# A mixture-of-experts layer whose experts' tokens are gathered two experts at a time

## The chip, the cores and the metric

The kernel runs on one core of a Trainium2 chip. The metric is device time in microseconds (us) of one execution. The core has five engines that run their own instruction queues: TensorE (PE in the profile; its weight loads are listed as PEld), VectorE (DVE), ScalarE (ACT), GpSimd (POOL) and SyncE (SP, which here only issues DMAs). TensorE's clock has two levels, 1.2 and 2.4 GHz; the profile gives the granted share of the higher one.

## The reference

Two transformer blocks of two layers each, on 256 tokens of 1024 channels, in float32. The change is in the second layer of the first block, whose feed-forward is a mixture of eight experts, two for each token:

```
def moe_swiglu(h, router_w, w1, w3, w2):
    logits = h @ router_w
    top_v, top_i = lax.top_k(logits, 2)
    probs = softmax(top_v)
    gates = sum(one_hot(top_i, 8) * probs[..., None], axis=-2)
    y = zeros_like(h)
    for e in range(8):
        y = y + gates[..., e:e + 1] * ((silu(h @ w1[e]) * (h @ w3[e])) @ w2[e])
    return y
```

w1 and w3 are 1024 x 2816 for each expert, w2 is 2816 x 1024.

## The kernel before

**Weights.** Every product is made of three: a float32 operand is held as a high and a low part of type fp32r, and `mm3` (lines 212 to 216) adds high x high, high x low and low x high. The weights arrive as float32 and are split on the core. `wload` (192 to 201) takes a staging slot, issues a 512 KB DMA on SyncE (line 198), casts the piece to its high part on ScalarE (199) and subtracts on VectorE to get the low part (200). There are six slots of split weights (`wh`, `wl`), and staging slots of two kinds: five (`ws`) for the whole kernel, and eleven more (`wx`) while the mixture layer runs. `stage` (181 to 187) hands them out in turn, by a counter `turn` that is set to 13 before the layer (line 1476). A staging slot is free again once the subtraction of line 200 has read it.

**Experts.** The one-hot matrix of an expert, tokens by slots, picks at most 128 tokens for the main pass. `collect(e)` makes these one-hot columns on VectorE (`select`, line 799, tile `pmr`), and `gather` (818 to 828) multiplies the tokens, held by rows as a high part (`hTh`) and a low part (`hTl`), with them: 8 channel blocks x 2 blocks of tokens x 2 parts are 32 matmuls with 128 moving columns, in two PSUM banks. The two banks go to `sink` (854 to 859): ScalarE applies the norm's scale and shift, one instruction for each channel block (858), and `split` makes the high and low part (lines 238 and 239). The result is held in a pair of four `y4` buffers, so that two experts' tokens are held at a time. `place` and `dispatch` (803 to 816) transpose the one-hot columns for the way back and make the gates.

**Order.** The loop of lines 915 to 933 goes over the experts and, in each, over six groups of hidden units (five of 512, one of 256). In a group, `first` multiplies the tokens with w1 and w3, and the group before it goes through `columns` (transposes, then a split) and `second` (the product with w2). `collect(e + 1)` stands at the end of the last group of expert e, between the product with w3 and `second` of the group before. A scheduler at build time arranges the instructions of each engine by the order in which they are written and by when their slots are free; on the chip each engine keeps that order.

**Memory.** PSUM holds four banks of the kind `mm` (gathers, first products, transposes) and four of the kind `acc`. The scratch kind `nrm` (`scr`) has six buffers of 4 KB on each partition. The eleven `wx` slots, the one-hot tiles and small tiles lie in a pool `experts` that takes the place of the mixer's pool.

**Before and behind the layer.** The output projection of the mixer (`w_out`) uses the `ws` slots. The first six pieces of expert 0 (the list PRE) are loaded and split before the router's result is known (line 1477). Behind the layer the next mixer uses `ws` slots alone.

Of the kernel before, what the change touches and what calls it, by code (L numbers as in the profile page):

```python
# [7 lines left out]
F32R = mybir.dt.float32r  # L8
# [18 lines left out]
# slots of staged weights, further ones in the MoE layer, slots of split weights  # L27
NWS, NEXTRA, NWH = 5, 11, 6
# the expert weights loaded before the router is known: matrix and first channel block
PRE = [("moe_w1", 0), ("moe_w1", 2), ("moe_w1", 4), ("moe_w1", 6), ("moe_w3", 0), ("moe_w3", 2)]  # L30
# pieces of the first weight loaded before the first operand is made
EARLY = 2
# adaptive-modulation pieces loaded per weight piece: mixers and feed-forwards in order
# [48 lines left out]
def table():  # L82
    """The small vectors, each by its name here, the input's name and index, and its columns of 128 channels."""
# [23 lines left out]
def layout(a):  # L107
    """The inputs as the kernel reads them: small vectors by columns, transposed views, zero-padded blocks."""
# [35 lines left out]
class Kern:  # L144
# [36 lines left out]
    def stage(self, shape):  # L181
        """A slot of the staged weights; the MoE layer's further slots take their turn."""
        n = NWS + (NEXTRA if self.extra else 0)
        self.turn = (self.turn + 1) % n
        if self.turn >= NWS:
            return self.t(self.extra, shape, "wx", bufs=NEXTRA)
        return self.t(self.wp, shape, "ws", bufs=NWS)
# [94 lines left out]
    def load_c(self, name):  # L282
        """A block's condition, in every partition."""
# [5 lines left out]
    def operand(self, shape=(P, 4, S)):  # L289
        """A split operand that a later product needs: its high and low parts."""  # L290
        return [self.t(self.xp, shape, "y4", F32R, 4) for _ in range(2)]
# [28 lines left out]
    def ada_unit(self, i, grp):  # L320
        """1024 channels of a layer's modulation: each staged piece holds 128 of them by rows."""
# [41 lines left out]
    def token_sums(self):  # L363
        """Each token's sum of squares, tokens on the partitions, in PSUM [P, 2]."""
# [10 lines left out]
    def token_rstd(self):  # L375
        """1 / rms of each token, broadcast over the partitions, in PSUM [P, S]."""
# [5 lines left out]
    def bcast(self, r):  # L382
        """[P, 2] per-token values to [P, S], the same in every partition, in PSUM"""
# [7 lines left out]
    def double_norm(self, g, gsc):  # L391
        """rms norm by g, then the statistics of a second rms norm of its result"""
# [27 lines left out]
    def scaled(self, gsc, rb, q):  # L420
        """The normed and scaled channel blocks 4 q to 4 q + 3."""
# [39 lines left out]
    def down(self, acc, src, r0, nk, aT, first, last):  # L461
        """acc (channel-major, [D, S]) += src[r0:r0 + nk * P]^T @ aT"""
# [12 lines left out]
    def hybrid(self, i, hT, mp):  # L475
# [5 lines left out]
        # attention outputs  # L481
        ogs = []

        def attend(t):
            """The rows of a block of tokens, normed and gated."""
# [19 lines left out]
        def columns(t):  # L505
            """Those rows by channels, split."""
# [6 lines left out]
        # forget gates  # L513
# [80 lines left out]
        # intra-chunk scores, transposed  # L594
# [14 lines left out]
        # recurrent branch input and convolution  # L609
# [13 lines left out]
        # gates of the recurrent branch  # L623
# [87 lines left out]
    def moe(self, sh, gsc, router, pools, mid):  # L711
# [5 lines left out]
        # tokens by rows and their norm: the channels' scale and shift are applied after the gather;  # L717
        # the router works on the tokens as they are: their norm's scale and shift are applied to its logits
# [47 lines left out]
        def tokens(q, ins):  # L766
            """Half the channels of the normed tokens, split; behind instruction ins."""
# [27 lines left out]
        def select(pool, e, base):  # L795
            """One-hot columns of the slots of expert e, from slot base on: [P, 2, P]"""
            mr = self.t(pool, (P, 2, P), "pmr", F32R, bufs=2)
            for t in range(2):
                self.selected = nc.vector.tensor_scalar(mr[:, t], self.c["slots"], float(base), pos[:, t, e:e + 1],
                                                        op0=ALU.add, op1=ALU.is_equal).ins  # L800
            return mr
# [16 lines left out]
        def gather(mr, sink):  # L818
            """The tokens of the slots, channel-major, handed to sink by banks."""
            for b in range(2):  # L820
                ps = self.bank("mm", (P, 4, P))
                for j in range(4):
                    cs = slice((b * 4 + j) * P, (b * 4 + j + 1) * P)
                    for t in range(2):
                        for z, part in enumerate((htH, htL)):
                            nc.tensor.matmul(ps[:, j], lhsT=part[:, t, cs], rhs=mr[:, t],
                                             start=(j == 0 and t == 0 and z == 0), stop=(j == 3 and t == 1 and z == 1))
                sink(b * 4, ps)

        def combine(mT, parts, h):  # L830
            """XT += gate * (one-hot)^T @ rows, rows given as parts that sum to them"""
# [15 lines left out]
        def collect(e):  # L847
            """The tokens of expert e."""
            mr = select(ep, e, 0)
            if e == 0:  # L850
                tokens(1, self.selected)
            xH, xL = self.operand((P, KC, P))

            def sink(k0, ps):
                x = self.scr((P, 4, P))
                for j in range(4):
                    k = k0 + j
                    nc.scalar.activation(x[:, j], ps[:, j], AF.Identity, bias=sh[:, k:k + 1], scale=gsc[:, k:k + 1])
                self.split(xH[:, k0:k0 + 4], xL[:, k0:k0 + 4], x)
# [694 lines left out]
```

## Time and profile before

| what | value |
|---|---|
| median of 3 runs | 2192.26 us (2190.09 to 2194.74) |
| span of the profiled execution | 2191.9 us |
| PE busy | 2095.2 us, 96% of the span |
| DVE busy | 1791.8 us, 82% |
| ACT busy | 1329.6 us, 61% |
| expert layer's products in that span | from about 493 us to 1290 us |

The profile is one execution with the hardware profiler on. It is 0.4 us shorter than the median of the three runs, so a sum made against its span stands for the runs as well. A matmul's listed duration overlaps that of the next one, so what a stream of matmuls costs is read from starts, not from durations. Idle time of an engine matters only where another engine, which has nothing else to do, waits for it.

### The profile page before, as it was taken

The numbers are of one execution on the slowest core, as the hardware profiler recorded it, in microseconds if no ns is written. First come the engines' busy times: TensorE is split into PE (matmuls) and PEld (weight loads), VectorE is DVE, ScalarE is ACT, GpSimd is POOL, SyncE is SP. The second block draws the span as 40 slices with busy tenths as digits, with TensorE's granted clock in tenths as the row PEclk, the third lists the DMA queues.
The fourth block names the chain that finished last, engine by engine and source line by source line (L and its number), as shares of the span: only waits on it lengthen the run. The fifth ranks groups of instructions, "written<-read, shape, count | busy, mean of one in ns | idle before, by whom it ended". The sixth has DMA issues, their size and how long they took to land. (4 is left out here: it accounts for less than half of the span.)

```text
span 2191.9 us, 36523 instructions
## 1 busy us (share of the span) xinstructions
PE 2095.2 (96%) x13990; PEld 1927.5 (88%) x13990; DVE 1791.8 (82%) x2509; ACT 1329.6 (61%) x1695; POOL 39.0 (2%) x49
## 2 busy tenths in 40 slices
PE   4979999989999999999999979999999999999998
PEld 4779998888888888888888869999999998999998
DVE  7988788878899999999898878867787777678765
ACT  3744444747878778787777655644555456346553
POOL 0000000000000000000000000000000000000000
PEclk9989999979999999999999989999999999899999
DMA  8778998778999999899999945756676556466762
GB/s 320 249 254 288 335 327 306 235 271 310 342 349 350 364 321 386 293 393 331 345 359 344 339 143 193 224 169 225 199 225 226 181 173 183 134 218 206 220 185 77
DMA packets 289926, 580.49 MB, mean 265 GB/s; under 512 B 17904, under 2 KB 47728, under 8 KB 289744
## 3 DMA queue, kind: packets, MB, share of 16 engines
q1 hardware_dynamic: 289024, 576.42, 76.7%
q8 instruction: 111, 1.82, 0.3%
q10 hardware_dynamic: 576, 1.21, 0.2%
q14 instruction: 71, 0.58, 0.1%
q0 software_dynamic: 144, 0.46, 0.1%
HBM read 576.97 MB, written 1.05 MB: 264 GB/s over the span
## 5 line engine op out<-in xcount | busy, mean ns | idle before, releaser
L199 ACT CAST wh<-ws 128x1024 fp32r<-128x1024 f32 x531 | 554.4, 1050 | 460.8 <-PE mm L215 171.0
L200 DVE TENSOR_TENSOR wl<-ws,wh 128x1024 fp32r<-128x1024 f32 x531 | 641.6, 1221 | 147.0 <-ACT wh L199 140.8
L214 PE MATMUL mm<-hTh,wh 128*128 128x256 f32 x1728 | 500.2, 291 | 27.0 <-ACT wh L199 20.7
L216 PE MATMUL mm<-hTh,wl 128*128 128x256 f32 x1728 | 498.6, 289 | 2.4 <-DVE wl L200 2.4
L215 PE MATMUL mm<-hTl,wh 128*128 128x256 f32 x1728 | 499.3, 289 | 0.0
L200 DVE TENSOR_TENSOR wl<-wx,wh 128x1024 fp32r<-128x1024 f32 x363 | 430.1, 1221 | 35.4 <-ACT wh L199 28.1
L199 ACT CAST wh<-wx 128x1024 fp32r<-128x1024 f32 x363 | 375.3, 1051 | 81.2 <-PE mm L216 52.8
L214 PEld LDWEIGHTS mm<-hTh,wh 128*128 128x128 f32 x1728 | 341.3, 198 | 31.4 <-ACT wh L199 20.9
L216 PEld LDWEIGHTS mm<-hTh,wl 128*128 128x128 f32 x1728 | 341.1, 197 | 3.2 <-DVE wl L200 2.9
L215 PEld LDWEIGHTS mm<-hTl,wh 128*128 128x128 f32 x1728 | 341.5, 198 | 0.7
L214 PE MATMUL mm<-wh,y 128*128 128x512 f32 (+1 forms) x768 | 290.6, 379 | 0.0
L215 PE MATMUL mm<-wl,y 128*128 128x512 f32 (+1 forms) x768 | 286.4, 373 | 0.8 <-DVE wl L200 0.8
L216 PE MATMUL mm<-wh,y 128*128 128x512 f32 (+1 forms) x768 | 285.8, 372 | 0.0
L332 DVE SCALAR_TENSOR_TENSOR ws<-ws,cb 128x1024 f32<-128x1024 f32 x192 | 232.9, 1219 | 45.2 <-DMA ws<-in_ada_w_dram 44.0
L214 PE MATMUL acc<-y,wh 128*128 128x256 f32 x736 | 208.8, 287 | 5.8 <-ACT y L242 5.8
L215 PE MATMUL acc<-y,wh 128*128 128x256 f32 x736 | 209.6, 285 | 0.6 <-DVE y L243 0.6
L216 PE MATMUL acc<-y,wl 128*128 128x256 f32 x736 | 209.4, 285 | 0.0
L215 PEld LDWEIGHTS mm<-wl,y 128*128 128x128 f32 x768 | 145.1, 189 | 26.3 <-DVE wl L200 2.7
L216 PEld LDWEIGHTS mm<-wh,y 128*128 128x128 f32 x768 | 144.8, 189 | 25.9
L214 PEld LDWEIGHTS mm<-wh,y 128*128 128x128 f32 x768 | 144.9, 189 | 24.1 <-ACT nrm L923 0.3
L214 PEld LDWEIGHTS acc<-y,wh 128*128 128x128 f32 x736 | 142.5, 195 | 6.1 <-ACT y L242 6.1
L215 PEld LDWEIGHTS acc<-y,wh 128*128 128x128 f32 x736 | 143.0, 194 | 0.9 <-DVE y L243 0.9
(399 smaller groups left out, 3045.0 us busy)
## 6 DMA issues: line engine op xcount, KB each, us to landing
wx<-in_moe_w_dram SPq DMA_DIRECT2D x363, 512.0 KB, 5.9
ws<-in_ada_w_dram SPq DMA_DIRECT2D x192, 512.0 KB, 4.6
ws<-in_moe_w_dram SPq DMA_DIRECT2D x165, 512.0 KB, 5.9
ws<-in_w_in_dram SPq DMA_DIRECT2D x116, 512.0 KB, 4.5
ws<-in_ffn_w_up_dram SPq DMA_DIRECT2D x88, 512.0 KB, 4.7
ws<-in_ffn_w_dram SPq DMA_DIRECT2D x66, 512.0 KB, 5.4
ws<-in_ffn_w_down_dram SPq DMA_DIRECT2D x44, 512.0 KB, 4.8
ws<-in_w_out_dram SPq DMA_DIRECT2D x32, 512.0 KB, 4.6
```

The source lines that it names most:

```text
L199: self.nc.scalar.copy(h, f)
L200: self.nc.vector.tensor_tensor(l, f, h, ALU.subtract)
L214: mm(out, lhsT=a[0], rhs=b[0], start=start, stop=False)
L215: mm(out, lhsT=a[0], rhs=b[1], start=False, stop=False)
L216: mm(out, lhsT=a[1], rhs=b[0], start=False, stop=stop)
L332: nc.vector.scalar_tensor_tensor(f, f, 1.0, c, op0=ALU.mult, op1=ALU.mult, accum_out=m[:, k:k + 1])
```

## The change

The tokens of experts 1 and 2, 3 and 4, 5 and 6 are gathered together, with 256 moving one-hot columns; experts 0 and 7 stay single. A gather of two is 32 matmuls, in four PSUM banks of two channel blocks each, drained by eight ScalarE instructions of 256 columns and four splits. It stands where the gather of the first of the two stood; `place` is still called for each expert at the end of the one before. Three experts' tokens are held: those of experts 0, 3 and 6 in two new buffers `xe` in the pool `experts`, the others in the four `y4` buffers. The one-hot tile has one buffer of 256 columns for each token block where there were two of 128. The further staging slots go from 11 to 9. `turn` still starts at 13; it is now taken modulo 14 where it was modulo 16, so the layer's first five pieces get the slots `ws`, where before its first two got `wx`.

The diff without changed comments and docstrings:

```diff
-NWS, NEXTRA, NWH = 5, 11, 6
+NWS, NEXTRA, NWH = 5, 9, 6
-        def select(pool, e, base):
-            mr = self.t(pool, (P, 2, P), "pmr", F32R, bufs=2)
-            for t in range(2):
-                self.selected = nc.vector.tensor_scalar(mr[:, t], self.c["slots"], float(base), pos[:, t, e:e + 1],
-                                                        op0=ALU.add, op1=ALU.is_equal).ins
+        def select(pool, es, base):
+            mr = self.t(pool, (P, 2, len(es) * P), "pmr", F32R, bufs=1)
+            for j, e in enumerate(es):
+                for t in range(2):
+                    self.selected = nc.vector.tensor_scalar(mr[:, t, j * P:(j + 1) * P], self.c["slots"], float(base),
+                                                            pos[:, t, e:e + 1], op0=ALU.add, op1=ALU.is_equal).ins
         def gather(mr, sink):
-            for b in range(2):
-                ps = self.bank("mm", (P, 4, P))
-                for j in range(4):
-                    cs = slice((b * 4 + j) * P, (b * 4 + j + 1) * P)
+            n = mr.shape[-1]
+            kb = 512 // n
+            for k0 in range(0, KC, kb):
+                ps = self.bank("mm", (P, kb, n))
+                for j in range(kb):
+                    cs = slice((k0 + j) * P, (k0 + j + 1) * P)
                     for t in range(2):
                         for z, part in enumerate((htH, htL)):
                             nc.tensor.matmul(ps[:, j], lhsT=part[:, t, cs], rhs=mr[:, t],
-                                             start=(j == 0 and t == 0 and z == 0), stop=(j == 3 and t == 1 and z == 1))
-                sink(b * 4, ps)
+                                             start=(j == 0 and t == 0 and z == 0), stop=(j == kb - 1 and t == 1 and z == 1))
+                sink(k0, ps)
-        def collect(e):
-            mr = select(ep, e, 0)
-            if e == 0:
+        def collect(*es):
+            mr = select(ep, es, 0)
+            if es[0] == 0:
                 tokens(1, self.selected)
-            xH, xL = self.operand((P, KC, P))
+            x = [self.operand((P, KC, P)) if e % 3 else [self.t(ep, (P, KC, P), "xe", F32R, 2) for _ in range(2)]
+                 for e in es]
+            half = {}
             def sink(k0, ps):
-                x = self.scr((P, 4, P))
-                for j in range(4):
+                if k0 % 4 == 0:
+                    half[k0 // 4] = self.scr((P, 4, len(es), P))
+                f = half[k0 // 4]
+                for j in range(ps.shape[1]):
                     k = k0 + j
-                    nc.scalar.activation(x[:, j], ps[:, j], AF.Identity, bias=sh[:, k:k + 1], scale=gsc[:, k:k + 1])
-                self.split(xH[:, k0:k0 + 4], xL[:, k0:k0 + 4], x)
+                    nc.scalar.activation(f[:, k % 4].rearrange("p e n -> p (e n)"), ps[:, j], AF.Identity,
+                                         bias=sh[:, k:k + 1], scale=gsc[:, k:k + 1])
+                if k % 4 == 3:
+                    for j, (xH, xL) in enumerate(x):
+                        self.split(xH[:, k - 3:k + 1], xL[:, k - 3:k + 1], f[:, :, j])
             gather(mr, sink)
-            cur[e] = dict(x=(xH, xL), mr=mr)
-            if e:
-                place(e)
+            for j, e in enumerate(es):
+                cur[e] = dict(x=x[j], mr=mr[:, :, j * P:(j + 1) * P])
                 if c0 + n == DFF and e + 1 < NEXP:
-                    collect(e + 1)
+                    if e + 1 not in cur:
+                        collect(*range(e + 1, min(e + 3, NEXP)))
+                    place(e + 1)
-                mr = select(fp, e, P)
+                mr = select(fp, (e,), P)
```

## Rows read from the trace of the kernel before

**Rows 1.** The page: busy time by engine; DMA share in 40 slices

```profile
PE 2095.2 (96%) x13990; PEld 1927.5 (88%) x13990; DVE 1791.8 (82%) x2509; ACT 1329.6 (61%) x1695; POOL 39.0 (2%) x49
...
DMA  8778998778999999899999945756676556466762
```

**Rows 2.** Windows of the expert layer: busy us (count), clock, DMA share, GB/s

```profile
600.00:700.00 100.00, 100.00 (x502) 84.48 (x501) 92.20 (x97) 79.95 (x92) 0.00 (x0) 1.00 0.96 350
...
900.00:1000.00 100.00, 99.53 (x498) 83.75 (x497) 93.76 (x99) 79.52 (x91) 0.00 (x0) 1.00 0.99 360
```

**Rows 3.** Waits from 500 to 1290 us: us in total, times, longest

```profile
ACT wh L199 <- PE mm L216: 72.4, 192, 2.2
...
PEld mm L215 <- DVE wl L200: 2.7, 5, 0.9
...
ACT wh L199 <- DMA wx<-in_moe_w_dram: 1.2, 4, 0.3
```

**Rows 4.** Waits of the DMA queue on SyncE from 500 to 1290 us

```profile
SPq L198 <- DVE wl L200: 519.8, 492, 5.4
```

**Rows 5.** Line 198, the weights' DMAs, from 500 to 1290 us

```profile
DMA to landing us min/median/max: 3.4/5.9/8.9
```

**Rows 6.** Windows around gathers, line 826 alone: PE, PEld, clock, DMA share, GB/s

```profile
580.00:585.00 5.00, 3.69 (x32) 3.66 (x32) 1.00 1.03 375
...
978.00:983.00 5.00, 3.69 (x32) 3.66 (x32) 1.00 1.05 404
```

**Rows 7.** Timeline of PE around expert 1's gather: start, duration, what

```profile
575.03 0.28 PE L215 MATMUL mm<-wl,y 128*128 128x256 f32 x1
...
580.53 0.28 PE L216 MATMUL mm<-wh,y 128*128 128x256 f32 x1
580.65 0.23 PE L826 MATMUL mm<-pmr,hTh 128*128 128x128 f32 x1
...
584.18 0.41 PE L247 MATMUL mm<-cst,pm 128*128 128x128 f32 x2
...
584.79 0.47 PE L214 MATMUL acc<-wh,nrm 128*128 128x512 f32 x1
...
590.13 0.39 PE L216 MATMUL acc<-wh,nrm 128*128 128x512 f32 x1
```

**Rows 8.** Timeline of ACT around the same gather

```profile
580.86 1.05 ACT L199 CAST wh<-wx 128x1024 fp32r<-128x1024 f32 x1 [0.39 <-PE mm L216]
582.59 1.51 ACT L858 ACTIVATE nrm<-mm,modt 128x128 f32<-128x128 f32 x4 [0.69 <-PE mm L826]
...
586.72 2.17 ACT L199 CAST wh<-ws 128x1024 fp32r<-128x1024 f32 x2
589.20 1.06 ACT L199 CAST wh<-ws 128x1024 fp32r<-128x1024 f32 x1 [0.30 <-PE acc L216]
```

**Rows 9.** Timeline of DVE around the same gather

```profile
587.80 5.07 DVE L200 TENSOR_TENSOR wl<-ws,wh 128x1024 fp32r<-128x1024 f32 x4 [0.26 <-ACT wh L199]
```

**Rows 10.** An ACT group by line and shape, whole span: busy, mean ns

```profile
L1414 ACT ACTIVATE ua<-mm,tab 128x256 f32<-128x256 f32 x44 | 21.4, 564 | 12.1 <-PE mm L216 12.1
```

**Rows 11.** Windows: the mixer's output projection, ahead of the layer

```profile
451.00:476.00 25.00, 25.00 (x199) 25.00 (x199) 17.68 (x25) 7.72 (x8) 0.00 (x0) 0.94 1.02 382
```

**Rows 12.** Timeline of SyncE's DMA issues in that stretch

```profile
449.68 1.41 SPq L198 DMA_DIRECT2D wx<-in_moe_w_dram  x2
...
454.03 0.37 SPq L198 DMA_DIRECT2D ws<-in_w_out_dram  x1
455.20 7.63 SPq L198 DMA_DIRECT2D ws<-in_moe_w_dram  x5
```

**Rows 13.** Timeline of ACT in that stretch

```profile
460.13 1.05 ACT L199 CAST wh<-ws 128x1024 fp32r<-128x1024 f32 x1 [3.34 <-DMA ws<-in_w_out_dram]
```

**Rows 14.** Timeline of SyncE at the layer's end

```profile
1267.62 1.51 SPq L198 DMA_DIRECT2D ws<-in_w_in_dram  x2
```

**Rows 15.** Timeline of ACT at the layer's end

```profile
1285.75 1.04 ACT L199 CAST wh<-ws 128x1024 fp32r<-128x1024 f32 x1
```

## The prediction

> **What bounds the kernel now.** The page comes first. Over the span TensorE is busy 96% of the time, more than any other engine, but in the slices of the expert layer the DMA share also stands at 8 or 9 tenths, so two limits are possible there [rows 1]. The windows of the layer sharpen this: TensorE is busy 99.5 to 100 of 100 us at a granted clock of 1.00, the 2.4 GHz level, VectorE 92 to 94, ScalarE 80, and the DMA engines are busy 96 to 99% of the time at 350 to 360 GB/s [rows 2]. The reader should not take the DMA share for the limit yet. The waits decide it. In the 790 us of the layer TensorE's weight loads wait 2.7 us for a split piece; ScalarE's casts wait 72.4 us for TensorE to give back a slot of split weights, and 1.2 us for a DMA [rows 3]. SyncE waits 519.8 us, 492 times, for the subtraction that frees a staging slot [rows 4]. So the loads stand ready and wait for room, the casts wait for TensorE, and TensorE waits for nobody. In this layer a microsecond taken from TensorE's instructions is a microsecond of the span, as long as its feeders keep ahead.
>
> **What the gathers cost TensorE.** The gather of expert 1 begins at 580.65 us and the next kind of matmul begins at 584.18: 3.53 us for 32 matmuls, 110 ns from one to the next [rows 7]. The other gathers behind the first cost the same: the windows around them show the same 3.69 us busy with 32 matmuls at full clock [rows 6]. There are seven of them, so 7 x 3.53 = 24.7 us. Expert 0's is single before and after and falls out.
>
> A matmul of 256 moving columns with the same 128 x 128 weights and the same type runs directly ahead of that gather: from 575.03 to 580.53 there are 46 steps, 120 ns each [rows 7]. Bounds for the new gather's matmul: not below 110 ns, since the weight load is the same and the columns are more; not above 220 ns, if time went by columns alone. I take 120 ns, the row with the same shape, weights and neighbourhood. A gather of two then costs 32 x 0.120 = 3.8 us. After the change there are three of these and one single (expert 7): 3 x 3.83 + 3.53 = 15.0 us. TensorE saves 24.7 - 15.0 = 9.7 us; at 110 ns it would be 10.6, at 220 nothing.
>
> One rule of the notes speaks against this. The row is that 128 columns cost 110 ns and 256 cost 120 [rows 7], so time does not go by columns. The Trainium skill, page "TensorE: Matmul & The Clock Gate", section "Back-to-back issue gap", gives the isolated gap as N / 2.4 + 2.5 ns, which is 56 ns at 128 columns and 109 at 256. By that estimate two single gathers would cost 3.57 us and one of two 3.50, and the whole change would save 0.2 us. This trace disagrees at 128 columns (110 ns, not 56). The same page's section "LDWEIGHTS" puts a load of 128 columns at 128 / 1.2 = 107 ns, with which the 110 ns agree.
>
> **ScalarE and VectorE at a gather.** ScalarE now handles one gather as follows: it finishes a cast begun at 580.86 (1.05 us), starts on the first bank at 582.59, and is back at casting at 586.72: 4.13 us, of which the eight instructions of line 858 are 2 x 1.51 and the two copies of the split the remaining 1.11 [rows 8]. A gather of two needs eight instructions of 256 columns; the same operation of that size, from PSUM, takes 0.564 us in another line [rows 10], so at most 4.5 us, and four copies at 0.56, 2.2 us: 6.7 us. It can start earlier, because a bank is full after 8 x 0.120 us instead of 16 x 0.110; from the cast's end at 581.91 it would run to 588.6, or 1.9 us later than now. What hides this is the store of split pieces. The cast at 580.86 waited for a slot that TensorE gave back as it ended the product with w3 [rows 8], so at the gather all six slots hold pieces for what follows. TensorE starts on the first at 584.79 and takes 24 matmuls to 590.13, 0.232 us each or 1.39 us for a piece [rows 7], so the seventh is wanted at 584.79 + 6 x 1.39 = 593.1. Its low part is ready at 587.80 + 5.07 / 4 = 589.1 [rows 9], 4.0 us early; after the change 2.1 us early. Cost: none. Without that cover it would be 1.9 us for each of three gathers, 5.7 us. The experts in between (2, 4, 6) come without this burst at all. VectorE makes as many selections and splits as before, four splits in a row instead of two; its queue behind them holds subtractions whose casts are late by the same 1.9 us, so it adds nothing.
>
> The one-hot tile has a single buffer now, so the selection for experts 3 and 4 waits for the readers of 1 and 2, the last of which is the copy in `place(2)`, an expert's time ahead: no cost. The buffers of tokens come free as early: expert 4's take those of expert 1, expert 5's those of expert 2. The four banks of a gather of two drain within the ScalarE stretch above, and the next use of the first two (in `place`) comes after they are drained: no cost.
>
> **Two staging slots fewer.** With 16 slots and 1.39 us for a piece a slot comes round in 22.2 us, with 14 in 19.5. It needs a landing of 5.9 us, 8.9 at worst [rows 5], a cast of 1.05 and a subtraction of 1.27 [rows 8, 9]: 8.2 us, 11.2 at worst. The reserve shrinks from 11.0 to 8.3 us in the worst case. No cost. The loads must also be a little faster: an expert is 66 pieces of 512 KB, 34.6 MB, which at 350 GB/s [rows 2] takes 98.9 us; 1.2 us less on average makes 354 GB/s. Single windows reach 404 GB/s [rows 6], so the loads have room.
>
> **Ahead of and behind the layer.** The order of slots changes. Before, two early expert loads went to `wx` slots and were issued at 449.68, ahead of the last `w_out` load at 454.03, while the DMA engines were full at 382 GB/s [rows 11, 12]; ScalarE waited 3.34 us for that load [rows 13], though TensorE was busy all 25 us [rows 11]. After it the first five go to `ws` slots, behind the `w_out` pieces that hold them. A load takes 512 KB / 382 GB/s = 1.37 us. If the last `w_out` load comes earlier by two, the gain is at most 2.7 us; if five expert loads slipped in front of it, the loss is at most 6.9 us. TensorE's busy window speaks for neither: I take zero. At the end the next mixer's first loads go out at 1267.62 and the first is cast at 1285.75 [rows 14, 15]. The last five expert pieces rather than the last nine will now be in `wx`, so the `ws` slots come free four pieces, 5.6 us, later: the load lands 18.1 - 5.6 - 5.9 = 6.6 us before its cast. No cost.
>
> **Sum.** 2191.9 - 9.7 = 2182.2 us for the profiled execution, whose span lies 0.4 us under the median of the runs: 2182.6 us.
>
> **Rivals.**
> Half covered: ScalarE's longer burst reaches TensorE in full, 3 x 1.9 us, as would be if VectorE (92% busy [rows 2]) could not catch up. 2182.6 + 5.7 = 2188.3 us. Against it stand the 2.1 us of reserve. 9%.
> Order at the start: expert loads get in front of `w_out`, up to 6.9 us: 2189.5. 7%.
> Transfers the limit: if 350 GB/s were all that the DMA engines can give, TensorE would save its 9.7 us only to wait for weights: 2192.3. For it stands a DMA share of 96 to 99% [rows 2]; against it, SyncE's 519.8 us of waiting for slots and the 404 GB/s. 6%.
> Cost by columns: 220 ns for a matmul of 256, nothing saved, 2192.3. Against it the 120 ns. The page's isolated gap, above, is this case. 3%.
> Slower: the slots run out. If loads were so late that the two missing slots are missed once in every expert, that is 2 x 1.39 us x 8 = 22.2 us, less 9.7: 2204.8. It decides from a landing time of 19.5 - 1.05 - 1.27 = 17.2 us on, twice the worst seen. 5%.
>
> **The numbers.** The forecast holds 70%, between 2179.9 (start gains 2.7) and 2186. The range 2179.5 to 2189.5 adds the half-covered case and most of the order at the start, and leaves out the other three. About 0.2%, 4.4 us, is what a measurement can tell from no change. Faster by more: the forecast and some of the two cases beside it, 80%. Within: the rest of those, the transfers and the columns, 14%. Slower: 6%.
>
> **What would show it.** In the changed trace, line 826's successor has 160 matmuls instead of 256, those of 256 columns 120 ns apart; TensorE stays busy 99% or more through the layer at full clock; its waits for `wl` stay near 3 us; the stretch from expert 0's products to the layer's end is about 9.7 us shorter, and the rest of the span is as before. The prediction is wrong if TensorE waits for a cast behind a gather of two, if ScalarE waits for DMAs, or if the stretch before 493 us changes by more than 1 us.

## The result: slower by 0.5%, and the profile after

The changed kernel took 2203.35 us, the median of five runs (2201.37 to 2207.95); the kernel before, beside it, 2194.74 us (2190.09 to 2196.58). The ratio is 1.0053, with a 95% interval from 1.0034 to 1.0072. The forecast was 2182.6 us. The profiled execution has a span of 2199.6 us, 7.7 us above that of before.

The page of the changed kernel (answers to [rows 1]):

```profile
span 2199.6 us, 36293 instructions
...
PE 2097.3 (95%) x13894; PEld 1915.4 (87%) x13894; DVE 1785.3 (81%) x2509; ACT 1304.0 (59%) x1671; POOL 39.0 (2%) x49
...
DMA  8778998668999999999999965646677645466652
```

There are 96 matmuls fewer, as the change says, and yet TensorE is busy 2 us longer. Its timeline around the gather of experts 1 and 2 (answers to [rows 7]) shows that the gather itself is as it was forecast:

```profile
583.24 0.28 PE L216 MATMUL mm<-wh,xe 128*128 128x256 f32 x1
583.36 0.28 PE L829 MATMUL mm<-pmr,hTh 128*128 128x256 f32 x1
...
587.03 0.28 PE L829 MATMUL mm<-pmr,hTl 128*128 128x256 f32 x1
587.15 0.38 PE L247 MATMUL mm<-cst,pm 128*128 128x128 f32 x2
```

From 583.36 to 587.15 are 3.79 us for 32 matmuls, 118 ns each (forecast: 3.83 us, 120 ns). To see where the time went after that, the starts of the same matmul are compared in both traces: the first matmul of each expert's product with w1, and the layer's last product.

| first product of | before, us | changed, less before | e5 | e9 |
|---|---|---|---|---|
| expert 0 | 493.11 | +1.0 | +0.3 | -0.5 |
| expert 1 | 590.50 | +2.9 | +2.2 | +1.1 |
| expert 2 | 689.68 | -0.6 | -1.4 | -2.4 |
| expert 3 | 788.85 | +1.7 | -1.1 | -2.1 |
| expert 4 | 888.04 | +2.8 | -3.5 | -5.7 |
| expert 5 | 988.64 | +8.1 | -1.9 | -3.9 |
| expert 6 | 1087.84 | +7.6 | -5.5 | -7.4 |
| expert 7 | 1187.49 | +11.6 | -4.8 | -7.9 |
| the layer's last product | 1285.65 | +11.6 | -4.2 | -7.5 |

(The columns e5 and e9 are two experiments, below.) Between experts 1 and 2 the changed kernel gains 3.5 us: that is the gather of expert 2, which is left out. (In e5, where nothing else covers it, the step at expert 6 is 3.6 us.) But from expert 2 on something takes more than the pairs give, 10.6 us in all from the layer's first product to its last. The waits of the layer, 500 to 1290 us, name it (us in total, times, longest; answers to [rows 3]):

```profile
ACT nrm L238 <- PE mm L247: 73.3, 28, 4.3
ACT nrm L933 <- PE mm L216: 57.3, 41, 2.7
...
ACT wh L199 <- PE mm L216: 29.0, 73, 2.2
...
PEld mm L215 <- DVE wl L200: 13.5, 20, 3.3
...
PEld acc L215 <- DVE wl L200: 5.6, 15, 0.5
...
ACT wh L199 <- DMA wx<-in_moe_w_dram: 1.5, 5, 0.3
```

TensorE waits 13.5 + 5.6 us for low parts of weights; taken over the whole layer, from 493 to 1300 us, it is 19.4 us, against 3.7 before. The transfers are not late: the casts wait 1.5 us for pieces in `wx` slots and 1.9 us for pieces in `ws` slots (before: 1.2 and 0.9). What changed is what ScalarE waits for. Before, it waited with a cast in hand for TensorE to give back a slot (72.4 us, [rows 3]); now that wait is down to 29.0 us, and ScalarE stands instead before the split of the transposed units (73.3 us) and before the silu (57.3 us). Before, these two were 25.2 and 22.9 us:

```profile
ACT nrm L238 <- PE mm L247: 25.2, 11, 4.1
ACT nrm L923 <- PE mm L216: 22.9, 40, 2.1
...
PEld acc L215 <- DVE wl L200: 1.0, 3, 0.4
```

A cast that has a slot and data stands in the queue behind them. ScalarE's timeline of the changed kernel in expert 2 shows it:

```profile
745.07 0.60 ACT L933 ACTIVATE nrm<-mm 128x512 f32<-128x512 f32 x1 [1.30 <-PE mm L216]
745.57 2.94 ACT L199 CAST wh<-ws 128x1024 fp32r<-128x1024 f32 x3
748.41 1.99 ACT L199 CAST wh<-wx 128x1024 fp32r<-128x1024 f32 x2
752.81 0.59 ACT L238 CAST nrm<-mm 128x512 fp32r<-128x512 f32 x1 [2.41 <-PE mm L247]
753.29 6.74 ACT L199 CAST wh<-wx 128x1024 fp32r<-128x1024 f32 x7
```

Five casts, then 2.41 us of standing until TensorE has transposed the units, then seven casts without a pause: the first of the seven, at least, could have begun earlier. The windows of the layer (us, PE busy, PEld, DVE, ACT, POOL, clock, DMA share, GB/s) show the same against [rows 2]:

```profile
600.00:700.00 100.00, 100.00 (x485) 83.87 (x484) 91.94 (x94) 77.77 (x83) 0.00 (x0) 1.00 1.00 360
...
800.00:900.00 100.00, 96.91 (x451) 78.07 (x450) 89.95 (x109) 69.58 (x80) 0.72 (x1) 0.98 0.96 338
900.00:1000.00 100.00, 98.88 (x485) 81.46 (x485) 88.32 (x96) 73.34 (x89) 0.00 (x0) 1.00 0.95 337
```

In the first window, with experts 1 and 2, TensorE is as busy as before; in the later ones TensorE, VectorE and ScalarE are all less busy, and so none of them has become the limit by its own work. What is left is the order in which their instructions stand.

**How far ahead the casts stand.** ScalarE and VectorE keep the order that the scheduler wrote at build time. So one can count, in each engine's list, how many casts of pieces that TensorE has not begun stand ahead of each split of transposed units (ScalarE), and likewise how many subtractions stand ahead of each product of silu and w3 (VectorE), from the first group of an expert to its sixth. These are counts in the instruction lists of the built programs, not times:

| kernel | splits, expert 2 | splits, expert 5 | VectorE, expert 2 | layer's first product to expert 7's, less before, us |
|---|---|---|---|---|
| before | 6 6 6 6 6 6 | 6 6 6 5 3 6 | 5 3 5 5 5 5 | 0 |
| changed | 4 3 2 1 1 1 | 5 4 3 1 1 1 | 3 2 2 1 1 1 | +10.6 |
| e1, e7 | 6 6 6 6 6 6 | 6 5 4 3 1 6 | 5 3 5 5 5 5 | +1.0, +4.8 |
| e2 | 5 5 5 5 5 5 | 6 5 5 5 5 5 | 5 4 5 5 5 5 | +16.5 |
| e3 | 5 5 4 2 1 5 | 4 4 2 1 1 1 | 4 4 3 2 1 1 | +13.3 |
| e4 | 7 6 6 6 6 6 | 7 6 6 6 5 6 | 5 4 5 5 5 5 | +6.8 |
| e5, e6 | 6 6 6 6 6 6 | 6 6 6 6 6 6 | 5 3 5 5 5 5 | -5.1, +1.4 |
| e8 | 6 6 6 5 3 3 | 5 4 3 1 1 6 | 5 3 5 4 3 2 | +11.6 |
| e12 | 5 5 5 5 7 5 | 6 5 5 5 7 5 | 4 4 3 2 1 3 | +19.4 |

The Trainium skill, page "PSUM — Partial Sum Buffer", section "Engine vs sequencer instructions", says that the queues of ScalarE and VectorE are strictly first in, first out. The 2.41 us of standing ahead of seven casts agree with it.

Expert by expert, TensorE's waits for low parts go with these counts. In the changed kernel they are 1.8, 3.9, 5.1, 3.2, 4.1 and 1.3 us in experts 2 to 7, and none in experts 0 and 1, where the splits still stand behind five or six casts. A count that falls to 1 late in an expert costs little if the expert began with six: this is so in the kernel before (experts 6 and 7), in e1 and e7 (experts 5 to 7) and in expert 7 of the changed kernel, and TensorE waits at most 1.3 us in each of these experts. Four long waits make up 8.3 of the 19.4 us, each where VectorE has other work to do first (two behind gathers, one with the rotary tables, one where an expert's result is added back); the other 32 take 0.2 to 0.5 us each.

### The profile page after: what moved, and what is told of

The parts are those of the page before. It is cut to its first block, busy times and chain, and to the rows that moved or that the text cites. A ratio compares the mean times of both kernels' runs of the same rounds, so it can differ in the third digit from the quotient of the medians.

```text
span 2199.6 us, 36293 instructions
## 1 busy us (share of the span) xinstructions
PE 2097.3 (95%) x13894; PEld 1915.4 (87%) x13894; DVE 1785.3 (81%) x2509; ACT 1304.0 (59%) x1671; POOL 39.0 (2%) x49
## 3 DMA queue, kind: packets, MB, share of 16 engines
HBM read 576.97 MB, written 1.05 MB: 263 GB/s over the span
## 5 line engine op out<-in xcount | busy, mean ns | idle before, releaser
L199 ACT CAST wh<-ws 128x1024 fp32r<-128x1024 f32 x556 | 574.7, 1050 | 448.0 <-PE mm L215 161.9
L200 DVE TENSOR_TENSOR wl<-ws,wh 128x1024 fp32r<-128x1024 f32 x556 | 668.4, 1219 | 163.7 <-ACT wh L199 160.8
L200 DVE TENSOR_TENSOR wl<-wx,wh 128x1024 fp32r<-128x1024 f32 x338 | 397.7, 1219 | 38.0 <-ACT wh L199 34.9
L199 ACT CAST wh<-wx 128x1024 fp32r<-128x1024 f32 x338 | 339.3, 1051 | 33.2 <-PE mm L216 18.3
L215 PE MATMUL mm<-wl,y 128*128 128x512 f32 (+1 forms) x480 | 180.8, 377 | 3.8 <-DVE wl L200 3.8
L214 PE MATMUL mm<-wh,y 128*128 128x512 f32 (+1 forms) x480 | 180.9, 377 | 0.0
L216 PE MATMUL mm<-wh,y 128*128 128x512 f32 (+1 forms) x480 | 179.2, 373 | 0.0
L216 PEld LDWEIGHTS acc<-y,wl 128*128 128x128 f32 x736 | 143.6, 195 | 0.0
L215 PE MATMUL acc<-wl,nrm 128*128 128x512 f32 x352 | 141.1, 401 | 0.2
L216 PE MATMUL acc<-wh,nrm 128*128 128x512 f32 x352 | 137.6, 391 | 0.0
```

What stands on the lines that cost most here:

```text
L199: self.nc.scalar.copy(h, f)
L200: self.nc.vector.tensor_tensor(l, f, h, ALU.subtract)
L214: mm(out, lhsT=a[0], rhs=b[0], start=start, stop=False)
L215: mm(out, lhsT=a[0], rhs=b[1], start=False, stop=False)
L216: mm(out, lhsT=a[1], rhs=b[0], start=False, stop=stop)
```

## The experiments

Theory O (order): the change makes the scheduler put silus and splits in front of casts, and the casts come late. Theory S (slots): two staging slots are missing while the kernel runs. Further suspects came up on the way: the new buffers of the tokens (experiments e9 to e11).

**e1: the slots alone.** The kernel before with 9 further slots.

```diff
-NWS, NEXTRA, NWH = 5, 11, 6
+NWS, NEXTRA, NWH = 5, 9, 6
```

> The kernel before with nine further staging slots instead of eleven, and nothing else. Theory O (the order of ScalarE's instructions, fixed when the kernel is built, lets fewer casts run ahead of the products): the count of casts that stand ahead of a group's silu falls to 2 or 3 from expert 4 or 5 on, one expert earlier than in the kernel before, so 2 to 5 us slower, by waits of TensorE for the low part, and no wait for a DMA. Theory S (two slots fewer starve the loads on the chip): most of the 7.7 us that the changed kernel lost is here already, and the casts wait for DMAs. A third way, that the slots cost nothing and pairing alone does it: same as before within 1 us.

Measured: 2193.8 us, ratio 1.0006 (0.9988 to 1.0023). TensorE waits 3.4 + 1.4 us for low parts. Two slots fewer cost nothing that can be measured, although the order already begins to fall in expert 3. The third way came true; the 2 to 5 us of theory O did not come: the counts fall as theory O says, but the store is full at the start of each expert and TensorE hardly waits.

**e2: the order written by hand.** The changed kernel, its loads, casts and subtractions written five pieces ahead, and silu, splits and product held behind the last cast or subtraction written.

```diff
+            while len(self.ahead) < AHEAD and self.future:
+                self.ahead.append(self.piece(*self.future.pop(0)))
...
-        self.nc.scalar.copy(h, f)
-        self.nc.vector.tensor_tensor(l, f, h, ALU.subtract)
+        self.cast = self.nc.scalar.copy(h, f).ins
+        self.sub = self.nc.vector.tensor_tensor(l, f, h, ALU.subtract).ins
...
-            self.split(aH[:, :nk], aL[:, :nk], ps[:, :nk])
+            with self.tc.issue_after(self.cast), self.tc.issue_after(self.sub):
+                self.split(aH[:, :nk], aL[:, :nk], ps[:, :nk])
...
+                    with self.tc.issue_after(self.cast):
+                        nc.scalar.activation(s[:, :n], h1[:, :n], AF.Silu)
...
+                with self.tc.issue_after(self.sub):
+                    nc.vector.tensor_tensor(s[:, :n], h3[:, :n], s[:, :n], ALU.mult)
```

> The changed kernel, slots and pairs as they are, with the loads and splits of five pieces written ahead of their product, and silu, the transposed units' split and the product with silu held behind the cast (ScalarE) or the subtraction (VectorE) of the piece written last; so five casts again stand ahead of each silu. Theory O: the waits behind the transposes go, TensorE is busy 99% or more again, and the layer is 15 to 20 us shorter than in the changed kernel: 2180 to 2187 us. Theory S: the same 14 slots, so no gain, 2198 to 2203. A third way, that the gathers of two cost more than the matmuls' 120 ns show: a gain of less than 10 us, with the loss at the three gathers of two.

Measured: 2207.38 us, 1.0068 (1.0047 to 1.0089). Its waits (TensorE's weight loads, the same stretch):

```profile
PEld mm L254 <- DVE nrm L960: 16.2, 5, 4.4
PEld mm L222 <- DVE wl L207: 3.1, 2, 2.9
```

The waits for low parts went, from 19.1 to 3.6 us in this stretch, as theory O says, and the time did not: it lies 20 us above the forecast of theory O. TensorE now waits for the product of line 960. The first of these five waits, 3.9 us in expert 0, comes from writing the loads ahead (e3 has it too, without the hold); the other four stand where the hold pushed the product back. VectorE's timeline at one of them:

```profile
799.11 6.89 DVE L207 TENSOR_TENSOR wl<-wx,wh 128x1024 fp32r<-128x1024 f32 x6
806.80 0.75 DVE L250 SCALAR_TENSOR_TENSOR nrm<-acc,sgate,nrm 128x512 fp32r<-128x512 f32 x1 [0.79 <-ACT nrm L249]
807.73 1.23 DVE L207 TENSOR_TENSOR wl<-wx,wh 128x1024 fp32r<-128x1024 f32 x1 [0.18 <-ACT wh L206]
808.88 0.68 DVE L960 TENSOR_TENSOR nrm<-mm,nrm 128x512 f32<-128x512 f32 x1
```

Seven subtractions run before the product that the transposes need. So this run undoes one wait and makes another, and its time does not decide. It shows, however, that the waits for low parts go with the order alone, with every load still on SyncE's queue.

**e3 and e4: the parts of e2.** e3 is the changed kernel with the loads written ahead, without the hold; e4 is the kernel before with all of e2's edit.

> The changed kernel with the loads and splits of five pieces written ahead of their product, as in e2_order, but nothing held behind anything. Theory O: the order that comes out has 2 or 3 casts ahead of silu from expert 2 on, as in the changed kernel, so the time is that of the changed kernel within 3 us, 2197 to 2203. If writing them earlier were what helps in e2_order, this would be as fast as that.

Measured: 2203.25 us, 1.0065 (1.0038 to 1.0092). Writing ahead alone leaves the order low (table) and the waits for low parts at 10.6 + 6.9 us.

> The kernel before with the order held as in e2_order. Theory O: before, the count ahead of silu falls to 2 only in experts 5 to 7, so little is to be had, 0 to 5 us: 2187 to 2194. Beside e2_order it gives what pairing is worth when the order is the same in both: 9.7 us by the sum of the prediction, 0 if pairing saves nothing.

Measured: 2200.82 us, 1.0027 (1.0007 to 1.0047), slower than the 2187 to 2194 us of the expectation: the edit costs the kernel before some 6 us. It does so through two waits for the product, 4.0 us in expert 0 and 2.3 us in expert 4; the first comes from writing ahead, as in e3. The hand-made order is worse than the scheduler's best one, so a better way to that one was needed.

**e5: another queue for half of the loads.** In the changed kernel every second expert load is issued on GpSimd's queue. That gives the scheduler two queues to plan with, and the splits stand behind six casts again in all experts (the table shows two of them), with no hold.

```diff
-        self.nc.sync.dma_start(out=f, in_=src.rearrange("(k p) n -> p k n", p=P))
+        q = self.nc.gpsimd if self.extra and self.turn % 2 else self.nc.sync
+        q.dma_start(out=f, in_=src.rearrange("(k p) n -> p k n", p=P))
```

> The changed kernel; while the layer runs every second weight load is issued on GpSimd's queue instead of SyncE's. The same loads, slots, pairs and engine work, but built this way five casts stand ahead of every silu and six ahead of every split of transposed units, in all eight experts, with nothing held by hand. Theory O: TensorE's waits for the low part fall from 19 us to below 4, and the layer is 14 to 18 us shorter than in the changed kernel: 2183 to 2189 us. If the order is not what costs, 2200 to 2206; if the second queue brings loads late, the casts wait for DMAs.

Measured: 2186.36 us (2181.28 to 2190.72), 0.9959 (0.994 to 0.9978): faster than before. Its waits in the layer:

```profile
ACT wh L200 <- PE mm L217: 91.5, 239, 2.2
...
ACT nrm L934 <- PE mm L217: 13.3, 40, 0.4
...
PEld mm L216 <- DVE wl L201: 3.2, 3, 1.2
```

ScalarE again waits with a cast in hand, the silu waits 13.3 us instead of 57.3, TensorE 3.2 us for low parts, all of it in expert 4, where VectorE also makes the rotary tables.

**e6: the same queues in the kernel before.**

> The kernel before with every second weight load of the layer on GpSimd's queue. The order comes out the same as in e5_queue. Theory O: the kernel before loses little by its order (3.7 us of waits for the low part), so 0 to 4 us faster, 2189 to 2193. Beside e5_queue, with the same order in both, it gives what pairing saves on the chip: 9.7 us by the sum of the prediction.

Measured: 2192.44 us, 0.9994 (0.9978 to 1.001). The second queue by itself is worth nothing that can be measured here. That it removed the waits in e5 through the order, and not by bringing loads sooner, is borne out by two other numbers: in the changed kernel the casts wait only 3.4 us for loads, and in e2 the waits for low parts go on one queue. Between e6 and e5, with the same order, the change is worth 6.1 us of the medians, and 6.5 us from the layer's first product to expert 7's (table). With the 3.6 us that the new buffers take (below) this comes near the 9.7 us of the prediction.

**e7: pairs undone.** The changed kernel with its 14 slots and new buffers, but single gathers.

```diff
-                        collect(*range(e + 1, min(e + 3, NEXP)))
+                        collect(e + 1)
```

> The changed kernel with the pairs undone: each expert gathered alone with 128 columns, but with the 14 slots, the single one-hot tile and the buffers xe. Theory O: the order is that of e1_slots, so the time is that of the kernel before, 2190 to 2196. A rival, that the buffers or the one-hot tile cost: as slow as the changed kernel.

Measured: 2195.53 us, 1.0008 (0.9988 to 1.0027); low parts 3.2 + 1.2 us. Without the pairs the order is that of e1 and the waits are nearly those of before (3.7 us). So the pairs bring the waits. What came with them is not free: the layer is 4.8 us longer than before (table), 1.2 to 1.7 us in each of the experts 0, 3 and 6, whose tokens lie in the new buffers.

**e8: the saved work given back.** The changed kernel with 32 unused matmuls of 128 columns at the end of experts 1, 3 and 5, 10.6 us of TensorE's time, and two small VectorE copies after each such block.

> The changed kernel with the time of the missing gathers given back: at the ends of experts 1, 3 and 5, where no gather is left, 32 matmuls of 128 columns with the expert's one-hot columns go into two banks that nobody uses. TensorE gets 10.6 us more work. The order comes out between the two kernels: the count ahead of silu recovers to 5 at experts 3 to 4, 5 and 7. Theory O: waits for the low part fall from 19 to 8 to 12 us, so the time stays about the same, 2199 to 2207, although TensorE does 10.6 us more. If the order is not what costs, 2212 to 2216.

Measured: 2205.15 us, 1.0054 (1.0035 to 1.0073), the changed kernel's ratio. Its waits:

```profile
PEld mm L215 <- DVE wl L200: 5.9, 13, 1.5
PEld acc L215 <- DVE wl L200: 2.8, 7, 0.4
```

With 10.6 us of extra work the waits are 10.4 us shorter (19.1 to 8.7), and the layer is only 1.0 us longer than in the changed kernel (table). TensorE's own work did not set the end in the changed kernel. The order rose in part too (table), so the run does not say which of the two shortened them.

**e12: ScalarE's order alone.** e2 with silu and splits held behind the cast only; the hold behind the subtraction is taken off the splits and the product.

```diff
-            with self.tc.issue_after(self.cast), self.tc.issue_after(self.sub):
+            with self.tc.issue_after(self.cast):
...
-                with self.tc.issue_after(self.sub):
-                    nc.vector.tensor_tensor(s[:, :n], h3[:, :n], s[:, :n], ALU.mult)
+                nc.vector.tensor_tensor(s[:, :n], h3[:, :n], s[:, :n], ALU.mult)
```

> The changed kernel with all loads on one queue, the loads written five ahead and ScalarE's silu and splits of the experts held in order behind the cast that was written before them, VectorE's product left free. Five casts stand ahead of each silu and five to seven ahead of each split of transposed units in all experts, against two to four and one to five in the changed kernel. Theory O (the order on ScalarE is the whole cause, the queue does nothing by itself): the waits of TensorE for low parts fall from 19.4 us to 4 or less and the layer comes to within 4 us of that of e5_queue; the whole comes to 2187 to 2193 us, since the loads written ahead cost some 3.5 us at the layer's start, as in e2_order. Rival (GpSimd's queue itself removed the waits in e5_queue): they stay, and the time is 2203 us or more. If TensorE waits for the products on VectorE instead, order on VectorE is what the hold by hand cannot give.

Measured: 2213.69 us, 1.0088 (1.007 to 1.0106), the slowest of all. Its waits:

```profile
DVE nrm L959 <- PE mm L223: 48.8, 21, 4.5
...
PEld acc L222 <- DVE wl L207: 11.0, 16, 2.6
```

Five to seven casts stood ahead on ScalarE, and the low parts were still late (11.0 us here and 3.8 us in the first products), because on VectorE, from expert 2 on, the product mostly stood behind only one to four subtractions and held up the rest (48.8 us). Theory O as I had put it, ScalarE alone, is wrong: the lead has to hold on both engines, as it does in e5 and, at the price of the product's waits, in e2.

**The pace of the new buffers.** The table of starts left some 1.2 us unexplained in each of the experts 0, 3 and 6. Twelve steps of 512 columns in expert 0, whose tokens lie in `xe`, and twelve in expert 2, whose tokens lie in a `y4` buffer, in the changed kernel:

```profile
503.43 0.40 PE L214 MATMUL mm<-wh,xe 128*128 128x512 f32 x1
...
506.23 0.40 PE L214 MATMUL mm<-wh,xe 128*128 128x512 f32 x1
...
743.28 0.39 PE L216 MATMUL mm<-wh,y 128*128 128x512 f32 x1
...
746.00 0.39 PE L216 MATMUL mm<-wh,y 128*128 128x512 f32 x1
```

2.80 us against 2.72: 233 ns and 227 ns for one. The tokens are the weights here, and in the built program `xe` begins at byte 216544 of each partition, which leaves 32 when divided by 64; `y4` begins at 157696, a multiple of 64.

**e9 and e10: 32 bytes of padding.** Ahead of `xe`, in e5's kernel and in the changed kernel. The pad also moves what lies in the same pools, above all the `wx` slots and the one-hot tiles, from 32 to 0 modulo 64:

```diff
+                self.nc.gpsimd.memset(self.t(mo, (P, 8), "pad"), 0.0)
```

> The kernel with every second weight load on GpSimd's queue (e5_queue: 2186.4 us, span 2186.8), and 32 bytes more ahead of the held tokens, so that the tokens of experts 0, 3 and 6 begin at a multiple of 64 bytes as those of the other experts do. Theory A (the address of the weights sets the pace): the 512-column matmuls of experts 0, 3 and 6, which step 233 to 234 ns in the changed kernel and 227 ns in the other experts, step 227 ns here, and with some 240 of them in each the layer is 3 x 1.2 us = 3.6 us shorter: 2182 to 2184 us. Rival R (the tile's place in the pool or the tokens copied by VectorE instead of by the gather's consumer set it, not the address): the step stays at 233 ns and the time at 2186 us.

Measured: 2180.9 us (2174.0 to 2185.3), 0.9935 (0.9917 to 0.9954), the best version of the study and somewhat below the 2182 to 2184 us expected. The layer accounts for part of this only: in the profiled execution it is 7.0 us shorter than before and the whole 19.7 us. The rest lies behind the layer, in stages that the edit does not touch, and single executions of the kernel before spread by as much (2181.6 to 2203.0 us).

> The changed kernel with the same 32 bytes and nothing else; the order of every engine's instructions is that of the changed kernel. Theory A: the pace in experts 0, 3 and 6 is 227 ns, the waits for the low parts of the weights stay (19.4 us in the layer), and the time is up to 3.6 us under the changed kernel's, 2199 to 2202 us, because where TensorE waits for a cast a faster matmul only lengthens the wait. Rival R: same pace and time as the changed kernel, 2203 us. If the waits for the low parts go with the pad, the theory that the order sets them is wrong.

Measured: 2201.44 us, 1.0036 (1.0022 to 1.005). Twelve steps of expert 0 in e10:

```profile
501.01 0.39 PE L216 MATMUL mm<-wh,xe 128*128 128x512 f32 x1
...
503.73 0.39 PE L216 MATMUL mm<-wh,xe 128*128 128x512 f32 x1
```

2.72 us, 227 ns: theory A holds. The `wx` slots and one-hot tiles that moved along do not set the pace: they begin at 32 modulo 64 in the kernel before, whose matmuls take 227 ns too. In e9 expert 3 and expert 6 are each 1.2 us shorter than in e5, expert 0 only 0.3 us (table of starts). In e10 the layer is only 1.1 us shorter than in the changed kernel. The waits for low parts are 14.4 + 6.0 us there, 1.3 us more in the same stretch, and behind two of them some fifteen matmuls of 512 columns ran near the lower clock level (granted clock 0.57 from 889 to 893 us and 0.53 from 1114.5 to 1118), where the changed kernel has five. So most of what the pace gave was lost again behind waits.

**e11: the other way round.** The kernel before with the tokens of all experts moved by 32 bytes (a pad ahead of `y4`). Here too the `wx` slots and the one-hot tiles move along, from 32 to 0 modulo 64.

> The kernel before, with the tokens of all eight experts moved by 32 bytes, so that they begin at a multiple of 32 and not of 64 bytes. Theory A: the 512-column matmuls of all eight experts step 233 to 234 ns in place of 227, and the layer is 8 x 1.2 = 9.6 us longer, 2200 to 2204 us. Rival R: the step stays at 227 ns and the time at 2193 us.

Twelve steps in expert 2 of e11:

```profile
741.39 0.40 PE L216 MATMUL mm<-wh,y 128*128 128x512 f32 x1
...
744.19 0.40 PE L216 MATMUL mm<-wh,y 128*128 128x512 f32 x1
```

2.80 us, 233 ns, and the layer is 9.5 us longer, as expected. The whole is not: 2192.77 us, 0.9993 (0.9977 to 1.0008), a miss. The kernel's other stages hold their tokens in the same four buffers, as the moving operand of 256 columns, and there the mean step fell from 120.2 to 117.7 ns (line `acc<-y,wh` behind the layer, 864 steps); with the stages ahead of the layer, where the median step of the same line fell from 120 to 117 ns (608 steps), this gives back most of the 9.5 us. So the shift slows one shape and speeds up another.

## Why the prediction was wrong, by its own steps

**Right.** A gather of two costs 3.79 us (3.83 forecast); the gather left out for expert 2 gives 3.5 us, and with the order restored (e5 against e6) the pairs give about what the sum said, less the pace of the new buffers; the load queue still waits for slots (526.6 us against the 519.8 of [rows 4]) and loads land in 5.6 us in the median, 8.3 at worst ([rows 5]: 5.9, 8.9); two staging slots cost nothing while the kernel runs (e1). ScalarE's burst at the gather was not sized too low either:

```profile
583.55 1.05 ACT L199 CAST wh<-wx 128x1024 fp32r<-128x1024 f32 x1 [0.35 <-PE mm L216]
584.51 2.45 ACT L866 ACTIVATE nrm<-mm,modt 128x256 f32<-128x256 f32 x5
...
590.33 1.14 ACT L238 CAST y<-nrm 128x512 fp32r<-128x512 f32 x2
```

From 584.51 to 591.4 are 6.9 us, with one cast of 1.05 among them, so 5.8 us without it; 6.7 were forecast as the most. This first burst, with the store still full, cost TensorE nothing.

**The step that failed** is "ScalarE and VectorE at a gather", with its "What hides this is the store of split pieces" and "so it adds nothing". It took the store of six pieces, 4.0 us of lead, from the trace of before and carried it into a kernel whose instruction order did not exist yet. Moving 32 matmuls and dropping two slots made the scheduler write another order from expert 2 on, and with it the store shrank from six to between five and one pieces ahead of a split (six again only at the ends of expert 6 and the start of expert 7). The step priced the burst against a cover that the change itself took away: the term that it put at nothing measured 15.7 us, TensorE's waits for low parts (19.4 us against 3.7).

The prediction's own sign of error came true. Right behind the second and the third gather of two, where the store was no longer full, TensorE waits 1.45 us each. VectorE, and then TensorE's weight loads, behind the second gather of two:

```profile
789.17 0.68 DVE L239 TENSOR_TENSOR xe<-nrm,xe 128x512 fp32r<-128x512 f32 x1
789.77 0.68 DVE L239 TENSOR_TENSOR y<-nrm,y 128x512 fp32r<-128x512 f32 x1
...
790.71 5.76 DVE L200 TENSOR_TENSOR wl<-ws,wh 128x1024 fp32r<-128x1024 f32 x5
```

```profile
791.98 0.19 PEld L215 LDWEIGHTS mm<-wl,xe 128*128 128x128 f32 x1 [1.45 <-DVE wl L200]
```

Two splits of the gather stand ahead of the subtraction that TensorE wants, so "it adds nothing" failed too. But these two waits are only 2.9 of the 19.4 us; TensorE waits for subtractions all through the experts, the longest time in expert 4, where VectorE also makes the rotary tables (sines and cosines for a later layer). TensorE's weight loads, and VectorE in the same stretch:

```profile
890.62 0.19 PEld L214 LDWEIGHTS mm<-wh,y 128*128 128x128 f32 x1
894.06 0.29 PEld L215 LDWEIGHTS mm<-wl,y 128*128 128x128 f32 x1 [3.26 <-DVE wl L200]
```

```profile
890.72 0.41 DVE L1023 SCALAR_TENSOR_TENSOR nrm<-nrm 128x256 f32<-128x256 f32 x1
...
892.80 1.21 DVE L200 TENSOR_TENSOR wl<-wx,wh 128x1024 fp32r<-128x1024 f32 x1
```

In the kernel before, where the splits of expert 4 stand behind five or six casts, TensorE waits for no low part longer than 0.9 us in the same stretch.

**The terms left out.** The new buffers were priced only by when they come free, not by their address: some 720 matmuls of 512 columns x 5.6 ns more, less 144 of 256 columns x 3 ns, is 3.6 us. At the layer's start seven matmuls ran at the lower clock level where three did before, 0.2 us each more: 0.8 us. Behind the wait of 3.26 us the clock fell again (windows; the clock follows the busy times):

```profile
890.00:894.00 4.00, 1.24 (x6) 0.66 (x4) 4.00 (x12) 1.35 (x2) 0.00 (x0) 0.94 0.82 289
894.00:897.00 3.00, 2.94 (x7) 2.36 (x8) 2.91 (x8) 2.65 (x4) 0.00 (x0) 0.51 0.60 173
```

Five matmuls at 0.51 of the clock, 0.2 us each more, add 1.0 us. In all: -9.8 for the pairs, +15.7 for waits for low parts (19.4 less 3.7), +3.6, +0.8, +1.0 give +11.3 us; measured, from the layer's first product to its last, +10.6. The span shows 7.7 us: the layer began 1.0 us late, and 3.9 us came back behind it, in stages that the change does not touch. Neither of these two is clear of the scatter between executions: in e10, whose order is the changed kernel's, the layer began 1.9 us early. So the zero that the prediction took for the start, where its rows spoke for neither side, is neither borne out nor refuted.

**The rivals.** None of the five named the cause in full. "Half covered" had a right place and, in VectorE, a right reason, but it came true only for the second and third pair, with 2.9 us of its 5.7; the order within every group, which took the rest, it did not have. "Slots run out" gave nearly the right time, 2204.8 us, by luck: its mechanism is late loads, and the casts wait 3.4 us for loads. "Cost by columns", with the isolated gap of the Trainium skill's page "TensorE: Matmul & The Clock Gate", section "Back-to-back issue gap", would have saved 0.2 us; the 3.5 us that a gather left out gives, and the 110 ns at 128 columns, where that gap is 56, speak against it. At 256 columns the measured 118 ns lie near its 109.

**Still open.** That the order falls because the scheduler's plan takes loads on one queue for the limit and TensorE overtakes them in it, is argued only: fewer slots (e1), less work on TensorE (changed against e7) and more of it (e8) move the counts in the direction that this would give, and a second queue (e5, e6) restores them. The plan itself was not looked into, and pairs with all 16 staging slots were not run, so what the two missing slots add to the fall of the order is open too. Nor is it known why the address matters, or why in opposite directions for the two shapes.

## What to carry to other kernels

Where a scheduler writes the engines' order, a slack read from a trace belongs to that order: after any edit, count again how many producers stand ahead of each consumer, on every engine of the chain, before a cost is called covered. A saving on the engine that sets the pace is worth only as much as its feeders' lead; here the same edit cost 0.5% with the lead lost and gave 0.4% with it restored. With the new buffers moved by 32 bytes as well the whole came out 0.65% faster, about half of that in the layer. An order forced by hand on one engine moves the wait to the next one.

## What the runs showed of the hardware that was not expected

Weights of 128 x 128 (fp32r) that begin 32 bytes off a multiple of 64 in each partition made a matmul with 512 moving columns take 233 ns in place of 227, in three experts of the changed kernel and in all eight of e11, and the padding took it back. With 256 columns it went the other way, about 117 ns in place of 120, whether the tokens were the weights (the 256-column groups of the experts) or the moving operand. Half of the weight loads issued by GpSimd did as well as all of them by SyncE (e6: 0.9994).
